# A hybrid transformer step: DMA stores begun on ScalarE, six load tiles for four, and one block inversion moved into the scan

## The chip, the cores and the metric

The kernel runs on one core of a Trainium2 chip. The metric is the device time of one execution in microseconds, median of three runs. The engines are called as the profile calls them: PE (TensorE), DVE (VectorE), ACT (ScalarE), POOL (GpSimd) and SP (SyncE, which here only begins DMAs).

## The reference, cut to what matters

Two trunk layers run over 128 context tokens and 1024 latent tokens of width 1024. Layer 0 has attention, layer 1 a bidirectional RWKV-7 mixer of 16 heads of 64; each ends with a squared-ReLU MLP. The change touches the mixer of layer 1 only:

```python
def wkv_scan(r, decay, k, v, kk, a, s0, reverse):
    def step(S, inp):
        r_t, w_t, k_t, v_t, kk_t, kka_t = inp
        sk = jnp.einsum('bhvk,bhk->bhv', S, kk_t)
        S = S * w_t[:, :, None, :] - sk[..., None] * kka_t[:, :, None, :] + v_t[..., None] * k_t[:, :, None, :]
        return S, jnp.einsum('bhvk,bhk->bhv', S, r_t)
    sf, ys = lax.scan(step, s0.astype(F32), seq, reverse=reverse)

def rwkv_mixer(h, p, s0):
    xr, xw, xk, xv, xa, xg = (h + xx * mu[n] for n in range(6))
    r = (xr @ w_rkv[0]).reshape(hs)
    k = (xk @ w_rkv[1]).reshape(hs)
    v = (xv @ w_rkv[2]).reshape(hs)
    g = jax.nn.sigmoid(xg @ g1) @ g2
    kk = (k * k_k).astype(F32)
    kk = kk * lax.rsqrt(jnp.sum(kk * kk, axis=-1, keepdims=True) + 1e-12)
    for d in range(2):
        wlog = -jax.nn.softplus(-(w0[d] + jnp.tanh(xw @ w1[d]) @ w2[d])) - 0.5
        decay = jnp.exp(-jnp.exp(wlog.astype(F32))).reshape(hs)
        a = jax.nn.sigmoid(a0[d] + (xa @ a1[d]) @ a2[d]).reshape(hs)
        kd = k * (1.0 + (a - 1.0) * k_a)
        y, sf = wkv_scan(r, decay, kd, v, kk, a, s0[:, d], reverse=(d == 1))
    ...
    out = (y.reshape(B, T, D) * g) @ w_o
```

## The kernel before, in words

All tokens are held as 1152 columns in three blocks of 384 (`TB`), the width as eight slices of 128 (`KD`); a slice holds two heads and is called a pair below. The scan is not run token by token but in 18 chunks of 64 tokens (`NC`), six (`NB`) to a block. Within a chunk the dependence of tokens on each other is a triangular matrix; its two 32x32 diagonal blocks are inverted by elimination (`invert`), the rest is products.

**`rwkv_proj` (about 2050 to 2775 us).** `dense` multiplies by the three weights in turn, k (i=1), r (i=0), v (i=2), in 24 pieces of one slice by one block each; a piece is 24 matmuls on PE, and its `done` function copies PSUM to an `ro` tile on ACT and stores it to DRAM: `out32` (L1114 to 1118) for k, r, v and the gate, `v_done` (L1203 to 1210) for v, which is also transposed and stored as `vtd`. During r and v, after every second piece, the generator `operands` (L1230) is advanced by one step. A step is one slice and one block, 24 in all: it loads k, kk and r from DRAM (`load`, L1223, tiles `ld`), multiplies kk on DVE (L1247), and for each direction builds the decay by tanh and exp on ACT (tiles `e` of `etiles`, or in three of four half-steps of the v phase slices of an idle activation buffer), a running sum on DVE (L1262), `ar` on POOL (L1270, 1271) and `bk` on DVE and POOL (L1278, 1279). It stores `ar` to `ard`, `bk` to `bkd`, and the masked diagonal blocks `nt`, which PE makes as `ng`, to `nd`. At a slice's last block `nd` becomes `self.tri[p8]`; for the first `PI` = 3 slices the pair's blocks are inverted at once (L1304): `invert` loads `iv`, runs 31 times two DVE operations (L1349, 1350), one ACT copy (L1352), and a store of `td` (L1354).

**`rwkv_scan` (about 2778 to 3502 us).** A list `plan` gives each generator's steps a due time and they are called in that order. For each pair p there are three `prepare`s (one per block), a `recurrence` of 54 steps and a `finish`; t = 27 p. The pairs with p >= `PI` are inverted at t-45 to t-25 (L1703), the context chunks' blocks (`KD`) at -12 to 8. `prepare` loads `ar`, `rp`, `bk` and, from `td`, the inverses `ta`; PE makes the 64x64 products `gp`, DVE masks them to `g` (L1454); then PE joins the diagonal inverses (`mp`, L1469, L1477) with ACT copies into `tt` (L1471). `recur` runs on two alternating pairs: PE `cp` (L1530), ACT `xt` (L1539), PE `cp` (L1546), ACT `mu` (L1548), PE `cp` (L1553), DVE sum (L1556).

**What orders the work.** All DMAs of these stages are begun on SP (`self.dma`). The framework's scheduler, which runs an own timeline, decides on which place of an engine's queue each instruction stands: an engine takes them strictly in that order. A tile pool with `bufs` buffers per tag makes a new tile wait for the last reader of the tile whose buffer it takes. Each DMA is put on one of eight lanes of semaphores (DMAHW0 to 7); the one that begins it first waits until the lane's previous DMA has landed.

The numbers that the change touches: `AB`, buffers of `ar` in `prepare` (L1425); `PI`; `EB`, buffers of `e` (L1221); `LB`, buffers of `ld` (L1224); and the `bufs=2` of `ta` (L1424).

Of the kernel before, what the change touches and what calls it, by code (L numbers as in the profile page):

```python
# [10 lines left out]
F32 = mybir.dt.float32  # L11
# [13 lines left out]
TB = 384  # L25
# [10 lines left out]
DW = (((1, "a"), (1, "b"), (2, "a")), ((2, "a"), (2, "b"), (3, "a")))  # L36
PVS = (2, 4)
GB = 8
AB = 4
GT = 22  # L40
MAN = 0
MB = 3
TTB = 5
SD = 0
YB = 3
PI = 3
PT = 27
EB, LB, KDE, OF, BKE = 7, 4, 1, 5, 1
PL = 13
NEK = 1  # L50
KO = 1
# [38 lines left out]
class Net:  # L90
    def __init__(self, tc, A, O, C):
        self.tc, self.nc = tc, tc.nc
        self.A, self.O, self.C = A, O, C
        nc = tc.nc
        self.V, self.S, self.G, self.T = nc.vector, nc.scalar, nc.gpsimd, nc.tensor
        self.dma = nc.sync.dma_start
        self.uid = 0

    def nm(self, s):
# [921 lines left out]
    def rwkv_proj(self, act, early, pool, pse, ps):  # L1021
        A, S, V, G, T, dma, dr = self.A, self.S, self.V, self.G, self.T, self.dma, self.dr
        KE = (V, G)[KDE]
        NC, NB = TOK // 64, 6
# [89 lines left out]
        def out32(dst, b, p):  # L1114
            o = pool.tile([128, TB], F32, tag="ro", name=self.nm("ro"), bufs=2)
            S.copy(o, p)
            dma(dst[:, b * TB : (b + 1) * TB], o)
            return o

        def head_sums(x, out):  # L1120
# [6 lines left out]
        def rows_out(out, src):  # L1127

            o, x = out.rearrange("k e (t p) -> (k e t) p", p=128), src.rearrange("p k e t -> p (k e t)")
            for i in range(0, x.shape[1], 72):  # L1130
                tp = pse.tile([128, HW], F32, tag="tp", name=self.nm("rtp"), bufs=3)[0:72, 0:128]
                T.transpose(tp, x[:, i : i + 72], self.ident)
                rt = load(None, "rt")[0:72, 0:128]
                S.copy(rt, tp)
                dma(o[i : i + 72], rt)

        def lowranks(n, hs, after):

# [63 lines left out]
        def v_done(p8, b, p):  # L1202
            o = out32(self.vd[:, p8], b, p)  # L1203
            for c in range(0, 6, 3):
                vp = pse.tile([128, HW], F32, tag="tp", name=self.nm("vp"), bufs=3)[0:64, 0:TB]
                for j in range(3):
                    T.transpose(vp[:, j * 128 : j * 128 + 128], o[:, (c + j) * 64 : (c + j) * 64 + 64], self.ident)
                vt = early.tile([128, TB], F32, tag="mix", name=self.nm("vt"), bufs=3)[0:64].rearrange("p (e c d) -> p e c d", e=2, d=64)
                S.copy(vt.rearrange("p e c d -> p c e d"), vp.rearrange("p (c e d) -> p c e d", e=2, d=64))
                dma(self.vtd[p8, :, :, 6 * b + c : 6 * b + c + 3], vt)  # L1210

        def etiles():

# [120 lines left out]
    def invert(self, pool, p):  # L1334
# [3 lines left out]
        V, S, dma, dr = self.V, self.S, self.dma, self.dr  # L1338
        n_ = self.tri[p]
        blocks = "a d c e i s t -> (a d c e i) s t" if p == KD else "d c e i s t -> (d c e i) s t"  # L1340

        both = pool.tile([128, 32, 2, 32], F32, tag="iv", name=self.nm("iv"), bufs=1)
# [8 lines left out]
            yield  # L1351
        S.copy(nb_, iv.rearrange("p x y -> p y x"))  # L1352
        t_ = self.tri[p] = dr.tile([*n_.shape[:-1], 2, 32], F32, name=self.nm("td"))
        dma(t_.rearrange(blocks.replace("s t", "s m t")), both)  # L1354


    def rwkv_scan(self, pool, late, ps, psl):
        A, S, V, G, T, dma, dr, O = self.A, self.S, self.V, self.G, self.T, self.dma, self.dr, self.O
        NC, NB = TOK // 64, 6
# [56 lines left out]
        def prepare(p, b, u):  # L1416

            for d in range(2):
# [2 lines left out]
                if self.tti[d] < TTB:  # L1421
                    G.memset(tt, 0.0)
                self.tti[d] += 1
                ta = u["ta", d, b] = pool.tile([128, NB, 2, 32], F32, tag="ta", name=self.nm("ta"), bufs=2)  # L1424
                ar = u["ar", d, b] = pool.tile([128, 3, NB, 64], F32, tag="ar", name=self.nm("ar"), bufs=AB)  # L1425
                bk = bks[self.bki % 2]
                rp = u["rp", d, b] = rps[self.rpi % GB]
# [57 lines left out]
        def recur(p, u, y):  # L1485

            k = p % 2
# [96 lines left out]
                T.transpose(fp[:, d], fm[:, d], self.ident)  # L1584
            S.copy(fs.rearrange("p d h k -> p d (h k)"), fp)
            for d in range(2):
                dma(O[6][0, 0, d, 2 * p : 2 * p + 2].rearrange("h v k -> v h k"), fs[:, d])

        def finish(p, y_):

# [300 lines left out]
```

## Time and profile before

| | us |
|---|---|
| three runs, median (lowest to highest) | 4452.35 (4450.34 to 4462.19) |
| the profiled execution, its own time | 4463.4 |
| its span in the profile | 4461.6 |
| PE busy (89% of the span) | 3987.0 |
| DVE busy (62%) | 2771.1 |
| ACT busy (38%) | 1711.8 |
| POOL busy (28%) | 1238.0 |

The profiled execution took 11.05 us more than the median of the three runs. The busy shares are means over stages that have different limits. The chain of waits that ended last, followed back from the end, is a PE chain (24% of the span on PE), and reaches back only to 3166 us; the stages that the change touches lie mostly ahead of that, so they are read from windows of time and from the waits of each engine in them.

### The profile page before, as it was taken

To read this page: it belongs to the slowest core of one execution; us is meant where nothing else is said; L and a number is where in the kernel's file an instruction comes from. 1 tells how busy PE (TensorE), PEld (TensorE's weight loads), DVE (VectorE), ACT (ScalarE), POOL (GpSimd) and SP (SyncE) were. 2 spreads that over 40 slices of the span, in tenths; PEclk is the share of its full clock that TensorE was granted. 3 is DMA by queue.
4 is the path that set the end of the run, shared out by engine and by line. 5 is a ranking of instruction groups with operands and counts; after the bars stand their busy time and mean duration, and the time that the engine had idled before them with its cause. 6 is when DMAs were issued, how large, how long until landed. Compare 5 with 4: busy or idle time off the path is not lost. (4 is left out here: it accounts for less than half of the span.)

```text
span 4461.6 us, 78674 instructions
## 1 busy us (share of the span) xinstructions
PE 3987.0 (89%) x30058; PEld 3386.6 (76%) x30058; DVE 2771.1 (62%) x5837; ACT 1711.8 (38%) x4041; POOL 1238.0 (28%) x1519
## 2 busy tenths in 40 slices
PE   6989998879999999978978686898898799999998
PEld 4767776667888888868966564676677589999997
DVE  6856788865766666675147885676653564444445
ACT  5436776543211121243344453354555342222122
POOL 1223557650000000024255575344444200000001
PEclk8999999889999999989988787898999699999999
DMA  4444223223222222221235666766553411111112
GB/s 163 128 139 119 76 73 89 79 68 124 77 73 70 74 79 67 75 98 47 100 110 142 168 206 168 168 149 153 137 143 104 175 62 48 38 48 43 43 38 99
DMA packets 558520, 452.36 MB, mean 101 GB/s; under 512 B 191302, under 2 KB 529214, under 8 KB 556990
## 3 DMA queue, kind: packets, MB, share of 16 engines
q1 hardware_dynamic: 558144, 447.33, 34.2%
q8 instruction: 238, 3.90, 0.4%
q14 instruction: 138, 1.13, 0.1%
HBM read 323.45 MB, written 123.76 MB: 100 GB/s over the span
## 5 line engine op out<-in xcount | busy, mean ns | idle before, releaser
L956 PE MATMUL acc<-w2h,f 128*128 128x512 f32 x2304 | 735.3, 393 | 4.8 <-ACT f L835 3.8
L936 PE MATMUL mp<-h_b,w1h 128*128 128x384 f32 x1536 | 521.9, 340 | 0.0
L936 PE MATMUL mp<-h_a,w1h 128*128 128x384 f32 x1536 | 517.1, 337 | 0.8 <-ACT h L300 0.7
L936 PE MATMUL mp<-h_a,w1l 128*128 128x384 f32 x1536 | 516.9, 337 | 0.0
L956 PEld LDWEIGHTS acc<-w2h,f 128*128 128x128 f32 x2304 | 433.1, 188 | 101.4 <-ACT f L835 5.5
L956 PE MATMUL acc<-w2l,f 128*128 128x512 f32 x1152 | 452.3, 393 | 0.0
L962 DVE TENSOR_TENSOR acc<-acc,acc 128x1024 f32<-128x1024 f32 x270 | 328.7, 1218 | 139.3 <-PE acc L956 136.9
L660 POOL TENSOR_TENSOR ptl<-pt,pth 128x512 fp32r<-128x512 f32 x192 | 248.2, 1294 | 219.8 <-DVE pth L659 129.0
L1453 PE MATMUL gp<-ar,bk 128*64 128x192 f32 x2304 | 290.7, 356 | 20.4 <-DMA bk<-bkd 11.5
L936 PEld LDWEIGHTS mp<-h_a,w1h 128*128 128x128 f32 x1536 | 288.5, 188 | 7.0 <-issue 2.0
L936 PEld LDWEIGHTS mp<-h_b,w1h 128*128 128x128 f32 x1536 | 289.0, 188 | 4.2 <-issue 0.7
L936 PEld LDWEIGHTS mp<-h_a,w1l 128*128 128x128 f32 x1536 | 289.2, 188 | 0.1
L938 ACT ACTIVATE mt<-mp 128x384 f32<-128x384 f32 x192 | 94.1, 490 | 501.2 <-PE mp L936 499.0
L1111 PE MATMUL rp<-mxh,pwh 128*128 128x384 f32 (+2 forms) x720 | 268.9, 374 | 10.2 <-POOL pwh L1102 6.1
L1111 PE MATMUL rp<-h_b,pwh 128*128 128x384 f32 (+2 forms) x720 | 261.2, 363 | 3.5 <-DVE h_b L1068 3.4
L988 POOL TENSOR_TENSOR acc<-acc,mraw 128x1024 f32<-128x1024 f32 x6 | 15.4, 2564 | 894.5 <-DVE mrv L110 887.9
L1111 PE MATMUL rp<-mxh,pwl 128*128 128x384 f32 (+2 forms) x720 | 258.4, 360 | 0.8 <-POOL pwl L1099 0.8
L956 PEld LDWEIGHTS acc<-w2l,f 128*128 128x128 f32 x1152 | 216.8, 188 | 44.9 <-issue 3.1
L1791 POOL MEMSET h_a<- 128x8 f32 x4 | 0.3, 113 | 901.3 <-PE mp L936 901.3
L1454 DVE TENSOR_TENSOR g<-gp,gm 128x384 f32<-128x384 f32 x288 | 157.6, 554 | 134.0 <-PE gp L1453 124.7
L940 DVE TENSOR_TENSOR mf<-mt 128x384 f32<-128x384 f32 x192 | 106.3, 553 | 214.4 <-ACT mt L938 214.4
L1453 PEld LDWEIGHTS gp<-ar,bk 128*64 128x64 f32 x2304 | 172.4, 146 | 45.7 <-DVE g L1454 10.7
(439 smaller groups left out, 9600.1 us busy)
## 6 DMA issues: line engine op xcount, KB each, us to landing
mraw<-in_mlp_w_dram SPq DMA_DIRECT2D x64, 1024.0 KB
adaw<-in_w_ada_dram SPq DMA_DIRECT2D x80, 512.0 KB
bkd<-bk SPq DMA_DIRECT2D x48, 384.0 KB
ard<-ar SPq DMA_DIRECT2D x48, 384.0 KB
q<-QSd SPq DMA_DIRECT2D x256, 64.0 KB
ar<-ard SPq DMA_DIRECT2D x40, 384.0 KB
praw<-in_rwkv_w_rkv_dram SPq DMA_DIRECT2D x24, 512.0 KB
x1d<-acc SPq DMA_DIRECT2D x18, 512.0 KB
```

The costliest lines, as they stand in the source:

```text
L660: (V if w < 4 else G).tensor_tensor(c["l"][:, g : g + w, o], t["tp", g][:, 0:w], f32(c["h"][:, g : g + w, o]), op=ALU.subtract)
L936: T.matmul(p, x[:, k, :], act[b].v[y][:, k], start=k == 0 and i == 0, stop=k == KD - 1 and i == 2)
L938: S.activation(t, p, AF.Relu)
L940: V.tensor_tensor(f, t, t, op=ALU.mult)
L956: T.matmul(p[:, hf], x[:, cols], y[:, n], start=j == 0 and i == 0, stop=j == 1 and i == 2)
L962: V.tensor_tensor(a, a, pf, op=ALU.add)
L988: (G if b < 2 else V).tensor_tensor(a, a, x1[t], op=ALU.add)
L1111: T.matmul(p, x[:, k, :], a[y][:, k], start=k == 0 and i == 0, stop=k == KD - 1 and i == 2)
L1453: T.matmul(gp[row(x), j].rearrange("p (a t) -> p a t", t=64), bk[e][:, x, q + j], ar[:, :, q + j], start=True, stop=True, tile_position=(0 ...
L1454: V.tensor_tensor(g[:, e].rearrange("p j a t -> p j (a t)"), gp, gm[:, d, e, None].to_broadcast([128, 2, 192]), op=ALU.mult)
L1791: net.G.memset(a.hx[:, :, z : z + 1], 0.0)
```

## The change

Three things are changed together.

First, 173 DMAs are begun by ACT (`nc.scalar.dma_start`) that were begun by SP: the stores of r and k (`rkd`, 48), of the gate (`gd`, 24), of v (`vd`, 24) and of its transpose (`vtd`, 48), the row sums (`kkd` 2, `bsd` 2), the inverses (`td`, 9) and the final states (16). SP keeps 1893 of its 2066. The stores of `ard`, `bkd`, `nd` and of the scan's output stay on SP.

Second, buffers: `ld` 4 to 6, `ta` 2 to 4, `e` 7 to 6, `ar` in the scan 4 to 3.

Third, `PI` 3 to 2: pair 2 is inverted in the scan's plan at t-45 to t-25 with t = 54, which is 9 to 29, rather than in the projections.

The counts of instructions on PE, DVE and POOL and of ACT's compute don't change. No PE instruction ahead of row 10508 of PE's 17,284 (rows of equal shape taken together) changes its place, and the last 4185 rows (the output projection and the last MLP) are the same.

```diff
-AB = 4
+AB = 3
...
-PI = 3
+PI = 2
...
-EB, LB, KDE, OF, BKE = 7, 4, 1, 5, 1
+EB, LB, KDE, OF, BKE = 6, 6, 1, 5, 1
...
         self.dma = nc.sync.dma_start
+
+        self.dma_s = nc.scalar.dma_start
...
             S.copy(o, p)
-            dma(dst[:, b * TB : (b + 1) * TB], o)
+            self.dma_s(dst[:, b * TB : (b + 1) * TB], o)
...
                 S.copy(rt, tp)
-                dma(o[i : i + 72], rt)
+                self.dma_s(o[i : i + 72], rt)
...
-                dma(self.vtd[p8, :, :, 6 * b + c : 6 * b + c + 3], vt)
+                self.dma_s(self.vtd[p8, :, :, 6 * b + c : 6 * b + c + 3], vt)
...
-        dma(t_.rearrange(blocks.replace("s t", "s m t")), both)
+        self.dma_s(t_.rearrange(blocks.replace("s t", "s m t")), both)
...
-                ta = u["ta", d, b] = pool.tile([128, NB, 2, 32], F32, tag="ta", name=self.nm("ta"), bufs=2)
+                ta = u["ta", d, b] = pool.tile([128, NB, 2, 32], F32, tag="ta", name=self.nm("ta"), bufs=4)
...
-                dma(O[6][0, 0, d, 2 * p : 2 * p + 2].rearrange("h v k -> v h k"), fs[:, d])
+                self.dma_s(O[6][0, 0, d, 2 * p : 2 * p + 2].rearrange("h v k -> v h k"), fs[:, d])
```

Line numbers of the changed kernel are higher by 2 from L98 on. Three places show how the instructions move.

**DVE, the operands' early steps.** Tiles kk_4375, kk_4408, kk_4473 are those of steps 1, 2 and 3. Before, from the last `bk` of step 1 to that of step 2's first half:

```order
L1278 SCALAR_TENSOR_TENSOR bk_4396_22217<-tha_4391_22201,en_4393_22205 128x384
L1247 SCALAR_TENSOR_TENSOR kk_4408_22320<-k_4407_22318,CB_103,kk_4408_22320 128x384
L1299 SCALAR_TENSOR_TENSOR kd_4384_22157<-r_4376_22134,CB_103,kd_4384_22157 128x384
L1292 TENSOR_TENSOR nt_4398_22246<-ng_4397_22221,nm_21929 128x192
L1262 SCALAR_TENSOR_TENSOR cum_4411_22326<-m01_19680,ec_4410_22325 128x390
L1125 COPY bss_21738<-hst_4399_22251 128x3x2
L1276 SCALAR_TENSOR_TENSOR tha_4413_22333<-tha_4413_22333,kk_4408_22320 128x384
L1278 SCALAR_TENSOR_TENSOR bk_4418_22349<-tha_4413_22333,en_4415_22337 128x384
```

Now, the rows from the last `bk` of step 0 on:

```order
L1280 SCALAR_TENSOR_TENSOR bk_4363_22028<-tha_4358_22012,en_4360_22016 128x384
L1301 SCALAR_TENSOR_TENSOR kd_4350_21966<-r_4342_21943,CB_103,kd_4350_21966 128x384
L1249 SCALAR_TENSOR_TENSOR kk_4408_22320<-k_4407_22318,CB_103,kk_4408_22320 128x384
L1294 TENSOR_TENSOR nt_4365_22057<-ng_4364_22032,nm_21929 128x192
L1127 COPY bss_21738<-hst_4366_22063 128x3x2
L1264 SCALAR_TENSOR_TENSOR cum_4378_22138<-m01_19680,ec_4377_22137 128x390
L1278 SCALAR_TENSOR_TENSOR tha_4380_22145<-tha_4380_22145,kk_4375_22132 128x384
L1280 SCALAR_TENSOR_TENSOR bk_4385_22161<-tha_4380_22145,en_4382_22149 128x384
```

The product kk of step n+1 stood right behind step n's last `bk`; now that of step n+2 stands there (kk_4408 behind step 0's bk_4363), so it runs a whole step ahead of its readers. The load of kk in SP's queue moves with it: kk_4473 stood behind step 2's first `bkd` store, and stands now behind step 1's last `ard` store.

**ACT, one step of the operands in the v phase.** The words in brackets are the semaphores that a row waits for (DMAHW0 to 7 are the lanes). Before:

```order
L1116 COPY ro_5009_25521<-rp_5008_25496 128x384 [waits DMAHW6_49,PE_49]
L1260 ACTIVATE es_4991_25378<-lp_4992_25380,hb_19683 128x384 [waits DMAHW1_49,DVE_49,PE_49]
L1264 ACTIVATE es_4991_25378<-lp_4993_25385,hb_19683 128x384
L1209 COPY vt_5011_25528<-vp_5010_25524 64x3x2x64 [waits DMAHW4_49,PE_49]
L1261 ACTIVATE es_4991_25378<-es_4991_25378 128x6x64 [waits Activation_49]
L1209 COPY vt_5013_25535<-vp_5012_25531 64x3x2x64 [waits DMAHW3_49,PE_49]
L1274 ACTIVATE es_4991_25378<-es_4991_25378,oka_19687,hb_19683 128x384 [waits Activation_49]
L1260 ACTIVATE es_4998_25431<-lp_4999_25433,hb_19683 128x384 [waits DMAHW5_49,DVE_49,Pool_49]
L1264 ACTIVATE es_4998_25431<-lp_5000_25438,hb_19683 128x384 [waits PE_49]
L1266 ACTIVATE es_4991_25378<-es_4991_25378 128x384 [waits DVE_49]
L1267 ACTIVATE es_4991_25378<-es_4991_25378 128x390 [waits Activation_49,Pool_49]
```

Now, at the same kind of place:

```order
L1211 COPY vt_4978_25429<-vp_4977_25425 64x3x2x64 [waits DMAHW0_49,PE_49]
L1211 COPY vt_4980_25436<-vp_4979_25432 64x3x2x64 [waits PE_49]
L1276 ACTIVATE es_4958_25279<-es_4958_25279,oka_19687,hb_19683 128x384 [waits Activation_49]
L1212 DMA vtd_19671<-vt_4978_25429 128x1x192 [waits DMAHW2_49,Activation_49]
L1266 ACTIVATE es_4965_25332<-lp_4967_25339,hb_19683 128x384 [waits PE_49]
L1212 DMA vtd_19671<-vt_4980_25436 128x1x192 [waits DMAHW4_49,Activation_49]
L1268 ACTIVATE es_4958_25279<-es_4958_25279 128x384 [waits DVE_49]
L1269 ACTIVATE es_4958_25279<-es_4958_25279 128x390 [waits Pool_49]
L1270 ACTIVATE Dc_11596<-es_4958_25279 128x6
L1268 ACTIVATE es_4965_25332<-es_4965_25332 128x384
L1269 ACTIVATE es_4965_25332<-es_4965_25332 128x390
L1270 ACTIVATE Dc_11596<-es_4965_25332 128x6
```

The two stores of vt and the one of ro stand between the tanh, exp and scaling operations of the operands, each with a wait for the ACT copy ahead of it and one for a DMA on its lane. Of the 173 stores 119 have such a lane wait, 102 of them for a DMA that SP began, most for `ard`, `bkd`, r, k and kk.

**PE, pair 2's first `prepare` in the scan.** mp_5517 is the product that reads the inverses of pair 2 (ta_5474) first. Before, and the row ahead of it:

```order
L1562 MATMUL yp_5448_28485<-g_5358_27750,mu_5406_28105 64x64
L1562 MATMUL yp_5448_28485<-g_5364_27791,mu_5406_28105 64x64 x2
L1453 MATMUL gp_5493_28827<-ar_5475_28730,bk01_27019 64x192 x4
L1469 MATMUL mp_5517_28982<-ta_5474_28729,g_5476_28739 32x32 x4
L1469 MATMUL mp_5517_28982<-ta_5474_28729,g_5485_28778 32x32
L1453 MATMUL gp_5499_28876<-ar_5497_28866,bk10_27020 64x192 x4
```

Now:

```order
L1555 MATMUL cp_5522_29017<-mu_5494_28849,g_5458_28541 64x64 x2
L1564 MATMUL yp_5504_28899<-g_5426_28330,mu_5494_28849 64x64
L1564 MATMUL yp_5504_28899<-g_5458_28541,mu_5494_28849 64x64 x2
L1548 MATMUL cp_5465_28600<-xt0_26961,tt03_26954 64x64 x2
L1548 MATMUL cp_5465_28600<-xt0_26961,tt13_26959 64x64 x2
L1471 MATMUL mp_5517_28982<-ta_5474_28729,g_5476_28739 32x32 x4
L1471 MATMUL mp_5517_28982<-ta_5474_28729,g_5485_28778 32x32 x4
L1471 MATMUL mp_5517_28982<-ta_5474_28729,g_5490_28817 32x32 x4
```

Before, it stood right behind the `gp` products of its own `prepare` (33 of the scan's 144 groups of `gp` stood ahead of it). Now 39 of them do, those of its `prepare` and the next half among them, and it stands behind rows of both running recurrences. On DVE the elimination of pair 2 now stands between `g` number 48 and number 70 of 288, where pair 3's stood (50 to 72); pair 3's moves to 78 to 89, ahead of where its first reader stands (108) by 19.

## Rows read from the trace of the kernel before

**Rows 1.** Windows: length, busy us of PE, PEld, DVE, ACT, POOL; clock, DMA share, GB/s.

```profile
2250.00:2550.00 300.00, 227.62 (x1929) 189.05 (x1927) 199.66 (x315) 131.91 (x279) 164.09 (x162) 0.83 0.49 138
2300.00:2350.00 50.00, 43.33 (x363) 35.99 (x360) 13.56 (x21) 16.30 (x35) 21.40 (x23) 0.80 0.45 135
2550.00:2600.00 50.00, 36.09 (x368) 28.62 (x368) 48.19 (x77) 21.87 (x48) 31.85 (x32) 0.76 0.64 196
2550.00:2780.00 230.00, 164.14 (x1984) 131.32 (x1984) 156.87 (x216) 106.45 (x238) 153.09 (x165) 0.79 0.62 189
2800.00:3500.00 700.00, 617.80 (x10483) 489.24 (x10483) 392.97 (x1045) 338.96 (x1111) 288.58 (x666) 0.90 0.55 135
```

**Rows 2.** Waits of DVE, 2255 to 2780 us: total us, times, longest.

```profile
DVE kk L1247 <- DMA kk<-kkd: 76.0, 19, 8.6
```

**Rows 3.** Timeline of DVE, two early steps: start, us, operation, [idle before].

```profile
2304.91 0.62 DVE L1247 SCALAR_TENSOR_TENSOR kk<-k,CB,kk 128x384 f32<-128x384 f32 x1 [6.71 <-DMA kk<-kkd]
...
2322.54 0.68 DVE L1276 SCALAR_TENSOR_TENSOR tha<-tha,kk 128x384 f32<-128x384 f32 x1 [2.05 <-ACT kd L1274]
2323.25 1.18 DVE L1278 SCALAR_TENSOR_TENSOR bk<-tha,en 128x384 f32<-128x384 f32 x1
2331.03 0.62 DVE L1247 SCALAR_TENSOR_TENSOR kk<-k,CB,kk 128x384 f32<-128x384 f32 x1 [6.60 <-DMA kk<-kkd]
2331.56 0.61 DVE L1299 SCALAR_TENSOR_TENSOR kd<-r,CB,kd 128x384 f32<-128x384 f32 x1
```

**Rows 4.** Timeline of SP in the second of them.

```profile
2323.28 0.54 SPq L1245 DMA_DIRECT2D kk<-kkd  x1
```

**Rows 5.** Waits of POOL, 2255 to 2780 us.

```profile
POOL ar L1270 <- DMA k<-rkd: 9.8, 1, 9.8
...
POOL ar L1271 <- DMA r<-rkd: 7.1, 1, 7.1
```

**Rows 6.** Waits of PE, 2255 to 2780 us.

```profile
PE hst L1124 <- DVE es L1299: 42.2, 11, 9.8
PE ng L1290 <- DVE bk L1278: 22.9, 9, 5.2
PE hst L1124 <- DVE kd L1299: 22.3, 7, 6.1
```

**Rows 7.** Three starts of kk on DVE around the third inversion.

```profile
2550.95 0.62 DVE L1247 SCALAR_TENSOR_TENSOR kk<-k,CB,kk 128x384 f32<-128x384 f32 x1 [5.40 <-DMA kk<-kkd]
...
2619.03 1.19 DVE L1247 SCALAR_TENSOR_TENSOR kk<-k,CB,kk 128x384 f32<-128x384 f32 x1 [2.84 <-DMA kk<-kkd]
...
2671.64 0.79 DVE L1247 SCALAR_TENSOR_TENSOR kk<-k,CB,kk 128x384 f32<-128x384 f32 x1 [3.29 <-POOL es L1298]
```

**Rows 8.** Windows of L1349, then L1350, in the third inversion: DVE busy us.

```profile
2540.00:2620.00 80.00, 18.96 (x31) 0.77 0.65 188
...
2540.00:2620.00 80.00, 20.38 (x31) 0.77 0.65 188
```

**Rows 9.** Source view of SP, 2000 to 2800 us: L1117 and L1210, durations in ns.

```profile
L1117 SPq DMA_DIRECT2D rkd<-ro x48: 319/320/2659, 2098.4 to 2434.4; - x48
...
L1210 SPq DMA_DIRECT2D vtd<-vt x48: 508/556/1749, 2465.9 to 2750.5; - x48
```

**Rows 10.** Waits of ACT, 2255 to 2780 us.

```profile
ACT vt L1209 <- DMA vtd<-vt: 8.0, 2, 7.7
```

**Rows 11.** Waits of ACT, 2800 to 3500 us.

```profile
ACT tt L1471 <- DMA ta<-td: 105.6, 33, 12.0
```

**Rows 12.** Waits of PE, 2800 to 3500 us.

```profile
PE yp L1562 <- ACT mu L1548: 20.3, 19, 5.4
PE cp L1546 <- ACT xt L1539: 19.0, 17, 5.6
PE mp L1469 <- DMA ta<-td: 9.7, 1, 9.7
```

**Rows 13.** Timeline of ACT: end of pair 3's inversion.

```profile
2923.87 1.96 ACT L1352 COPY iv<-iv 128x1024 f32<-128x1024 f32 x1
```

## The prediction

> **What bounds the kernel now.** I read the windows of time first, to see which engine is full in which stage, then each engine's waits in the two stages that the change touches, then a few steps one by one. The chain of waits is of no use here: it reaches back only to 3166 us.
>
> In the projections' stretch with the operands (2250 to 2780 us) no engine is full for long [rows 1]: PE is busy 227.6 of 300 us and then 164.1 of 230, so 138 us of it are idle in all, DVE 199.7 and 156.9, ACT 131.9 and 106.5. The bound moves: from 2300 to 2350 us PE is busy 43.3 of 50 us and DVE 13.6, while from 2550 to 2600 us, under an inversion, DVE is busy 48.2 and PE falls to 36.1. The reader is to see a chain that passes from load to DVE to PE and back: DVE waits 76.0 us in 19 places for the load of kk [rows 2], and PE waits 42.2 + 22.3 + 22.9 = 87.4 us for DVE's products behind it [rows 6]. PE's granted clock averages 0.83 and 0.79 in these two windows, a mix of its levels of 2.4 and 1.2 GHz, against 0.90 in the scan, where PE is fuller [rows 1]; what a fuller PE would get back in clock has no term.
>
> In the scan (2800 to 3500 us) PE is busy 617.8 of 700 us [rows 1], so 82 us are idle at most. ACT waits 105.6 us in 33 places for the loads of `ta` [rows 11], and PE waits 20.3 + 19.0 us behind ACT's copies and 9.7 us for `ta` itself [rows 12].
>
> **The change part by part.** Gains have a minus.
>
> *kk's load, 4 to 6 `ld` tiles.* Before, the load of kk is begun at 2323.28 us [rows 4] and DVE uses it at 2331.03 [rows 3]: 7.75 us, of which the last `bk` of the step before covers 1.18 and the wait is 6.60. Now the load goes out behind the last `ard` store, and kk's product behind the product of bonus sums (L1301). Between issue and use then lie `tha` (0.68), `bk` (1.18), that product (0.61) and, I take, half of the 2.05 us that `tha` waits for ACT: 3.5 us in all. What is left to wait is 4.3 us for 6.6, 35% less, and 35% of 76.0 is **-27**. From both sides: 0, if the load's buffer comes free no earlier against its use than now; -76, if it lands in time every time. I take the value near the low end, since load and use moved ahead together, a full step each.
>
> *k and r.* POOL waits 9.8 us for k and 7.1 us for r, once each [rows 5]; with two more tiles both loads go out sooner. **-10**, between -17 and 0.
>
> *The third inversion.* Its 62 operations take DVE 18.96 + 20.38 = 39.3 us [rows 8]. The four steps that it lies in take 2619.03 - 2550.95 = 68.1 us, the four after it 2671.64 - 2619.03 = 52.6 us [rows 7]: **-15.5**; between -39, all of it, and 0, if the later steps are short for another reason. In the scan it lies beside DVE's other work, where DVE is busy 393.0 of 700 us [rows 1], so its operations are covered; its lateness has a term below. If that cover went, it would give back up to 39 us.
>
> *Stores begun by ACT.* A store of r, k or v costs the beginning engine 0.32 us, one of `vtd` 0.556 [rows 9]. In the v phase that is 24 x 0.32 + 48 x 0.556 = 34.4 us on ACT, which is busy 106.5 of 230 us [rows 1], 46%. With that share of it on the path it is **+15**. Queued behind a store on ACT are the tanh and exp of the operands, for which DVE's running sum and POOL's `ar` wait; what a lane wait adds there is the second rival. From below: ACT waits 8.0 us, 7.7 of them once, for `vt` tiles whose stores SP had not begun [rows 10]; with ACT itself beginning them that can go, so -8 to +78 (worked out with that rival). SP loses those issues, but it is no bound: it took kk's load within 0.03 us of the start of the `bk` beside it [rows 3, 4].
>
> *`e` tiles 7 to 6.* Matters in the first nine steps, 18 half-steps, where all half-steps use these tiles. The spare tile lets the next half-step start one operation early; nearest row is `bk` with 1.18 us [rows 3], so 0 to 18 x 1.18 = +21. I take **+5**: the reader that holds the tile, POOL's `ar`, runs ahead of `bk`.
>
> *`ta` 2 to 4.* At most the 20.3 + 19.0 + 9.7 = 49 us by which PE waits behind ACT or `ta` [rows 12], at least nothing. **-15**, a third: many of the 33 waits are for an inverse that has just been stored, which buffers don't hasten.
>
> *`ar` 4 to 3 in the scan.* Loads of `ar` start a half later; the nearest row of a late load is PE's one wait for `ta`, 9.7 us [rows 12]. 0 to +20 (two of them), taken as **+5**.
>
> *Pair 2's inverse late.* Its elimination takes the place in DVE's order where pair 3's stood. That one ended with an ACT copy at 2923.87 + 1.96 = 2925.8 us [rows 13]; a store and a load follow, at kk's 7.75 us each about 2941. Pair 2's first `mp` stood at `g` 66 of 288, six before pair 3's last operation at 72; at 700 / 288 = 2.4 us a `g` that was about 2909, so it comes some 30 us later. PE has `gp` of two halves and two recurrences to run meanwhile: 0 to +30, taken as **+6**, near the low end for that cover. What is late next is the ACT copies to `tt` of that pair, and its recurrence.
>
> *Stores of `td` and final states on ACT.* 22 after the second inversion, at 0.32 us [rows 9]: 0 to +7, **+2**.
>
> The sum: -27 - 10 - 15.5 + 15 + 5 - 15 + 5 + 6 + 2 = **-34.5 us**. Against the profiled execution's 4463.4 us that is 4428.9. The profiled execution was 11.05 us above the median of the runs, 4452.35, so on that I forecast 4417.9, rounded **4418**.
>
> **The rivals.**
>
> *All loads hidden.* If six tiles take kk, k and r off DVE's and POOL's path, the terms are -76 and -17 for -27 and -10: -34.5 - 56 = -90.5, 4362 us. For it: 87.4 us of PE's waits lie behind DVE's chain [rows 6], and 138 us of PE are idle. Against: kk's use in DVE's order moved as far ahead as its load.
>
> *ACT stalls at its stores: slower.* Place: the v phase. A store waits on ACT until its lane's earlier DMA has landed, and 102 of the 119 lane waits are for DMAs that SP began, which take up to kk's 7.75 us. From 2550 to 2780 us ACT has 230 - 106.5 = 123.5 us free. Of the 72 v stores that begin in the 285 us from 2465.9 to 2750.5 [rows 9] some 58 fall there, with 28 us of issue, so 96 us or 1.65 us a store can be lost before ACT is full. At a mean wait of 3 us ACT is 58 x 3 - 96 = 78 us over; in place of the +15 above the sum is -34.5 - 15 + 78 = +28.5, 4481 us. It decides from 58 x 2.5 = 145 us of lane waits on, a mean of 2.5 us. For it: ACT is in order, and the operands of DVE and POOL stand behind. Against: the lane's earlier DMA is eight begins back, mostly landed.
>
> *No change.* kk's product waits as before, because the loads gain nothing: 0 for -27, so -7.5 or 4445 us. For it: 7.75 us lie between begin and use however SP is filled, and SP's queue is not what holds the load [rows 3, 4].
>
> The Trainium skill has a rule that speaks for this one ("DMA: Bandwidth & Descriptors", section "Issuing engines are not separate DMA queues"): beginning DMAs on several engines saves only the sequencer's time to begin them, as all run on the same 16 engines. By it the move of the stores alone would be worth nothing to the loads, which the row of kk's load bears out as far as it goes.
>
> **How the numbers follow.** Chances: the forecast 0.42, all hidden 0.18, ACT stalls 0.17, no change 0.23. The likeliest case alone runs from 4395 to 4440 by the ends of its small terms. The range for 8 in 10 goes on down into the case of hidden loads and up to near the slower rival: 4365 to 4475 us. A measurement of this kernel tells 0.3%, 13 us, from no change, so faster is below 4439 and slower above 4466. Faster: all of the hidden loads' 0.18, 0.40 of the forecast and 0.03 of no change, 0.61. Same: 0.18 of no change, 0.02 of the forecast, 0.01 of ACT's stalls, 0.21. Slower: 0.16 of ACT's stalls and 0.02 of no change, 0.18.
>
> **What would show it.** In the changed profile DVE's wait for kk should be near 50 us (near 10 by the first rival, 76 by the third); the four steps that held the inversion should take about 53 us; ACT should show no wait for the store of `vt`; ACT's lane waits ahead of its stores should sum to under 50 us (over 145 by the second rival); in the scan ACT's wait for `ta` should fall from 105.6 to some 70 us, with one long wait for pair 2's. The prediction is wrong if the operands' stretch does not get shorter by 30 us or so, or if the scan gets longer by more than 15.

## The result, and the profile after

The changed kernel takes 4436.06 us (median of 8 runs, 4430.76 to 4440.16), the kernel before 4460.59 us in the same series (8 runs, 4450.34 to 4469.76). The ratio is 0.9946, 95% interval 0.9933 to 0.9959: faster by about 24 us. One execution of a kernel further down (the best version, 4623.2 us at a granted clock of 0.81, where its others have 0.93 to 0.94) was in a slow state and is in none of the times and ratios. The forecast was 4418 us, 34.5 us less than before; of the two profiled executions the changed one spans 32.6 us less (4429.0 for 4461.6). The sum came out near the forecast; several of the terms of which it was made did not, and the runs below are about that.

The page of the changed kernel: its span, the busy time of the engines, and a DMA queue that the kernel before does not have.

```profile
span 4429.0 us, 78546 instructions
...
PE 3958.8 (89%) x30058; PEld 3373.4 (76%) x30058; DVE 2748.4 (62%) x5837; ACT 1711.2 (39%) x4041; POOL 1237.2 (28%) x1519
...
q10 hardware_dynamic: 24672, 33.71, 2.3%
```

The queue q10 is new and carries ACT's stores, 33.7 of the 447 MB. The engines' work is the same in kind and count; PE's busy time fell from 3987.0 to 3958.8 us, while the mean granted clock of the two profiled executions rose from 0.929 to 0.937.

Where the time went is read best from one line: the recurrence's first product `cp`, whose first and last start mark when the scan's recurrences begin and end. The source view of that line, before, then after (durations in ns, first and last start in us):

```profile
L1530 PE MATMUL cp<-mu,g x1152: 219/222/369, 2804.1 to 3497.3; 128*64 128x64 f32 x192
```

```profile
L1532 PE MATMUL cp<-mu,g x1152: 219/222/368, 2773.2 to 3465.0; 128*64 128x64 f32 x192
```

The first `cp` comes 30.9 us earlier, the last 32.3: all but 1.4 us of the gain lies ahead of the scan, and the scan from first to last `cp` takes 691.8 us for 693.2. The windows of the same stretches as [rows 1], same columns:

```profile
2250.00:2550.00 300.00, 224.97 (x2023) 186.22 (x2022) 206.32 (x322) 138.90 (x294) 174.44 (x172) 0.84 0.51 148
2300.00:2350.00 50.00, 47.01 (x415) 38.50 (x414) 16.67 (x27) 20.33 (x43) 27.83 (x26) 1.00 0.52 152
2550.00:2600.00 50.00, 39.25 (x490) 30.45 (x490) 30.30 (x39) 23.60 (x53) 39.27 (x40) 0.88 0.67 201
2550.00:2780.00 230.00, 168.72 (x2060) 133.88 (x2062) 125.51 (x200) 100.11 (x232) 149.00 (x173) 0.81 0.68 190
2800.00:3500.00 700.00, 602.97 (x10113) 480.94 (x10108) 417.42 (x1083) 342.64 (x1101) 285.54 (x639) 0.90 0.57 141
```

In the early steps, 2300 to 2350 us, PE is busy 47.0 of 50 us for 43.3 and its granted clock is 1.00, that is 2.4 GHz throughout, for 0.80, a mix with 1.2 GHz. Under the place where the third inversion was, 2550 to 2600, DVE's 48.2 us became 30.3. In the last window the scan had begun by 2773.

DVE's waits in 2255 to 2780 us, after; the first answers to [rows 2]:

```profile
DVE kk L1249 <- DMA kk<-kkd: 88.9, 22, 10.1
...
DVE nt L1294 <- PE ng L1292: 6.2, 4, 3.9
```

DVE's wait for kk did not fall from 76.0 to 50, as forecast; it is 88.9. (Of such a difference some 14 us can be chance: the kernel c below, whose projections hold the same operations of DVE in the same order as before, has 62.3.) What fell is its wait for PE's `ng`, which in the kernel before was

```profile
DVE nt L1292 <- PE ng L1290: 26.1, 5, 8.4
```

and PE's waits for DVE's products, 29.9 + 24.6 + 8.3 = 62.8 us for [rows 6]'s 87.4:

```profile
PE ng L1292 <- DVE bk L1280: 29.9, 11, 6.0
PE hst L1126 <- DVE es L1301: 24.6, 10, 5.0
...
PE hst L1126 <- DVE kd L1301: 8.3, 5, 4.8
```

An early step shows both. DVE's timeline, after, answering to [rows 3]:

```profile
2301.59 0.62 DVE L1249 SCALAR_TENSOR_TENSOR kk<-k,CB,kk 128x384 f32<-128x384 f32 x1 [4.82 <-DMA kk<-kkd]
...
2307.81 0.36 DVE L1294 TENSOR_TENSOR nt<-ng,nm 128x192 f32<-128x192 f32 x1 [0.80 <-PE ng L1292]
2311.26 0.97 DVE L1264 TENSOR_TENSOR_SCAN cum<-m,ec 128x390 f32<-128x390 f32 x1 [3.09 <-POOL ec L1261]
...
2318.83 0.62 DVE L1301 SCALAR_TENSOR_TENSOR kd<-r,CB,kd 128x384 f32<-128x384 f32 x1 [2.98 <-POOL ec L1261]
2324.06 0.62 DVE L1249 SCALAR_TENSOR_TENSOR kk<-k,CB,kk 128x384 f32<-128x384 f32 x1 [4.61 <-DMA kk<-kkd]
```

and SP's begin of that step's kk:

```profile
2316.76 0.58 SPq L1247 DMA_DIRECT2D kk<-kkd  x1
```

The step from kk to kk is 2324.06 - 2301.59 = 22.5 us; before it was 2331.03 - 2304.91 = 26.1. The wait for kk inside it is 4.61 us for 6.60, close to the 4.3 that was worked out, and 7.3 us still lie between the load's begin and its use. A larger change is another: `nt` now waits 0.80 us for `ng`. In the kernel before the same `nt`, of the step's second half, was:

```profile
2319.25 0.36 DVE L1292 TENSOR_TENSOR nt<-ng,nm 128x192 f32<-128x192 f32 x1 [6.98 <-PE ng L1290]
```

There PE had a dense piece ahead of `ng` in its queue: `ng` began at 2318.58 us, 6.3 us after the `bk` that it reads was done. Of these 6.2 us less for `ng` and 2.0 less for kk only 3.6 are left in the step, since DVE now waits 3.09 and 2.98 us for POOL's `ec`, where it had no such wait.

### The profile page after: what moved, and what is told of

Read it like the earlier page. It is cut to its first block, busy times and chain, and to the rows that moved or that the text cites. A ratio compares the mean times of both kernels' runs of the same rounds, so it can differ in the third digit from the quotient of the medians.

```text
span 4429.0 us, 78546 instructions
## 1 busy us (share of the span) xinstructions
PE 3958.8 (89%) x30058; PEld 3373.4 (76%) x30058; DVE 2748.4 (62%) x5837; ACT 1711.2 (39%) x4041; POOL 1237.2 (28%) x1519
## 5 line engine op out<-in xcount | busy, mean ns | idle before, releaser
L990 POOL TENSOR_TENSOR acc<-acc,mraw 128x1024 f32<-128x1024 f32 x6 | 15.3, 2558 | 894.1 <-DVE mrv L112 887.5
L1456 DVE TENSOR_TENSOR g<-gp,gm 128x384 f32<-128x384 f32 x288 | 157.3, 554 | 105.6 <-PE gp L1455 98.3
```

Of the source, the lines that this page charges most:

```text
L1456: V.tensor_tensor(g[:, e].rearrange("p j a t -> p j (a t)"), gp, gm[:, d, e, None].to_broadcast([128, 2, 192]), op=ALU.mult)
```

## The experiments

All ratios are to the kernel before in the same series. There are three series, each on another chip, with five to twelve executions of each kernel: one for the four kernels with one part undone, one for the four with one part alone, one for the pairs and the last experiment. The edits are named by a letter each: **s**, stores begun by ACT; **t**, the projections' tiles (`ld` 6, `e` 6); **c**, the scan's tiles (`ta` 4, `ar` 3); **p**, pair 2 inverted in the scan (`PI` 2). The changed kernel is s+t+c+p.

| kernel | ratio (95%) | first cp, us | scan, first to last cp, us |
|---|---|---|---|
| before | 1 | 2804.1 | 693.2 |
| p | 1.0006 (0.9995 to 1.0018) | 2791.6 | 691.2 |
| s | 1.0008 (0.9996 to 1.0021) | 2813.2 | 680.9 |
| t | 1.0002 (0.9991 to 1.0014) | 2801.0 | 692.5 |
| c | 0.9988 (0.9977 to 0.9999) | 2807.6 | 670.9 |
| t+c | 0.9963 (0.9951 to 0.9976) | 2800.4 | 672.0 |
| s+c | 0.9964 (0.9951 to 0.9976) | 2809.6 | 662.2 |
| s+t | 0.9967 (0.9955 to 0.9979) | 2781.6 | 685.7 |
| s+t+c | 0.9928 (0.9907 to 0.9948) | 2783.7 | 669.7 |
| t+c+p | 0.9952 (0.9936 to 0.9969) | 2794.9 | 672.9 |
| s+c+p | 0.9970 (0.9956 to 0.9984) | 2796.0 | 676.4 |
| s+t+p | 0.9965 (0.9951 to 0.9978) | 2772.6 | 695.6 |
| s+t+c+p | 0.9946 (0.9933 to 0.9959) | 2773.2 | 691.8 |

The last two columns are from one profiled execution of each kernel. How far they can be trusted is seen in the five pairs of rows that differ by c alone, which changes tiles of the scan only: their first `cp` differ by 0.6 to 3.6 us. The stretch behind the last `cp`, which no edit was meant to touch, takes 963.9 to 971.7 us in these kernels. And p's profiled execution, 4454.4 us, was the fastest of its twelve, whose median is 4462.7.

### One part undone

The inversion back in the projections (s+t+c):

```diff
-PI = 2
+PI = 3
```

> The changed kernel with PI = 3 again: pair 2's inversion is back in the projections, all else as changed. The changed kernel stands at 0.9946 of before. Theory 1 (the inversion's removal from the projections is the largest term, and costs nothing in the scan): 10 to 16 us come back, all between 2500 and 2780 us, ratio 0.997 to 0.998; first cp of the scan 10 to 16 us later than the changed kernel's 2773.2. Rival 1 (the inversion is covered in both places; the tiles and stores carry the gain): ratio 0.994 to 0.996. Rival 2 (pair 2's late inverse costs the scan as much as the projections gain): ratio 0.994 to 0.996 with first cp 10 us later and the scan 10 us shorter.

It ran in 4425.44 us, 0.9928: none of the 10 to 16 us of theory 1 came back, and the ratio is 1.8 parts in a thousand, 8 us, under the changed kernel's, though the two intervals touch. The first `cp` is 10.5 us later, in the range of theory 1, but the scan is 22.1 us shorter:

```profile
L1532 PE MATMUL cp<-mu,g x1152: 219/222/371, 2783.7 to 3453.4; 128*64 128x64 f32 x192
```

That is rival 2's kind, and more than it asked. Why the projections gave less than the inversion's 39 us is seen in five steps of DVE's kk. With the inversion beside them (s+t+c):

```profile
2542.00 0.61 DVE L1249 SCALAR_TENSOR_TENSOR kk<-k,CB,kk 128x384 f32<-128x384 f32 x1
...
2554.84 0.61 DVE L1249 SCALAR_TENSOR_TENSOR kk<-k,CB,kk 128x384 f32<-128x384 f32 x1
...
2568.01 0.59 DVE L1249 SCALAR_TENSOR_TENSOR kk<-k,CB,kk 128x384 f32<-128x384 f32 x1
...
2584.47 0.60 DVE L1249 SCALAR_TENSOR_TENSOR kk<-k,CB,kk 128x384 f32<-128x384 f32 x1
...
2597.26 1.02 DVE L1249 SCALAR_TENSOR_TENSOR kk<-k,CB,kk 128x384 f32<-128x384 f32 x1
...
2618.86 0.62 DVE L1249 SCALAR_TENSOR_TENSOR kk<-k,CB,kk 128x384 f32<-128x384 f32 x1 [4.39 <-DMA vtd<-vt]
```

and in the changed kernel, with none:

```profile
2539.85 0.62 DVE L1249 SCALAR_TENSOR_TENSOR kk<-k,CB,kk 128x384 f32<-128x384 f32 x1 [4.25 <-DMA kk<-kkd]
...
2553.30 0.62 DVE L1249 SCALAR_TENSOR_TENSOR kk<-k,CB,kk 128x384 f32<-128x384 f32 x1 [1.93 <-DMA kk<-kkd]
...
2564.57 0.62 DVE L1249 SCALAR_TENSOR_TENSOR kk<-k,CB,kk 128x384 f32<-128x384 f32 x1 [2.58 <-DMA vtd<-vt]
...
2578.66 0.62 DVE L1249 SCALAR_TENSOR_TENSOR kk<-k,CB,kk 128x384 f32<-128x384 f32 x1 [4.68 <-DMA kk<-kkd]
...
2595.30 1.30 DVE L1249 SCALAR_TENSOR_TENSOR kk<-k,CB,kk 128x384 f32<-128x384 f32 x1 [2.54 <-DMA kk<-kkd]
...
2610.64 0.62 DVE L1249 SCALAR_TENSOR_TENSOR kk<-k,CB,kk 128x384 f32<-128x384 f32 x1 [5.27 <-DMA kk<-kkd]
```

The first four steps take 55.3 us with the inversion's operations on DVE and 55.4 without. With them DVE is busy for 54.7 us of that, without them for 34.0, and it waits at the kk of each step, three times for kk's load and once for `vtd`, 11.7 us in all. The fifth step, in which the inversion ends, does get shorter, from 21.6 to 15.3 us. Over the stretch DVE's wait for kk in s+t+c is

```profile
DVE kk L1249 <- DMA kk<-kkd: 48.7, 14, 9.4
```

so taking some 39 us of work off DVE [rows 8] put 40 us of waiting there, 88.9 for 48.7. In all five pairs of kernels with and without p this wait is longer with p, by 22 to 47 us.

The stores back on SP (t+c+p):

```diff
-        self.dma_s = nc.scalar.dma_start
+        self.dma_s = nc.sync.dma_start
```

> The changed kernel with all 173 stores begun by SP again. Theory 1 (the forecast's term: a store on ACT costs its issue, 15 us on the path in the v phase, and gives the loads nothing): faster than the changed kernel by some 15 us, ratio about 0.991. Rival 1 (SP's queue held loads behind stores that waited for ACT's copies, and that is the gain): 15 to 30 us come back, ratio 0.998 to 1.001, with DVE's wait for kk and ACT's wait for vt longer. Rival 2 (neutral, both terms small): 0.994 to 0.996.

0.9952, rival 2: neutral in time. But not stage by stage: the first `cp` comes 21.7 us later and the scan is 18.9 us shorter than in the changed kernel. In the projections that is what rival 1 asked, with DVE's wait for kk at 98.8 us, though ACT's wait for the stores of `vt` did not come back.

The projections' tiles as before (s+c+p):

```diff
-EB, LB, KDE, OF, BKE = 6, 6, 1, 5, 1
+EB, LB, KDE, OF, BKE = 7, 4, 1, 5, 1
```

> The changed kernel with 4 ld tiles and 7 e tiles again. Theory 1 (the forecast's terms for kk, k, r and e: -27, -10, +5): 32 us come back, ratio about 1.002. Rival 1 (DVE's wait for kk did not shrink in the changed kernel, 88.9 us for 76.0, so the tiles are worth nothing): ratio 0.994 to 0.996. Rival 2 (the tiles gain not through the wait for kk but through the order: ng ahead of the dense products on PE in the first nine steps, where DVE's wait for ng fell from 26.1 to 6.2 us): 10 to 20 us come back, ratio 0.997 to 0.999, and DVE's wait nt<-ng is over 20 us again.

0.9970: 11 us came back, at the low end of rival 2 and with intervals that touch. DVE's wait of `nt` for `ng` is 18.8 us again, just short of the 20 that this rival asked. Theory 1's 32 us did not come back.

The scan's tiles as before (s+t+p):

```diff
-AB = 3
+AB = 4
...
-                ta = u["ta", d, b] = pool.tile([128, NB, 2, 32], F32, tag="ta", name=self.nm("ta"), bufs=4)
+                ta = u["ta", d, b] = pool.tile([128, NB, 2, 32], F32, tag="ta", name=self.nm("ta"), bufs=2)
```

> The changed kernel with the scan's tiles as before: ta 2, ar 4. Theory 1 (the forecast's terms -15 and +5): 10 us come back, all in the scan, ratio about 0.997, ACT's wait for ta about 100 us again. Rival (the scan is bound by the recurrence and PE, and ta's loads by the inverses, not the buffers; it took 692 us in both kernels): ratio 0.994 to 0.996, though ACT's wait for ta is long again.

0.9965: 8 us came back by the ratio, where theory 1 asked 10, though with intervals that touch, and in the profile only 3.8 us of it lie between first and last `cp`; the stretch behind the last `cp` is 7.7 us longer, inside its scatter in the other kernels.

### One part alone, on the kernel before

The same four edits, each made alone on the kernel before.

p alone:

```diff
-PI = 3
+PI = 2
```

> The kernel before with PI = 2 alone: pair 2's inversion moves to the scan, nothing else. Theory now (from the changed kernel with PI = 3: first cp 10.5 us later, scan from first to last cp 22.1 us shorter, in all 8 us faster): the move gains 10 to 16 us in the projections and costs the scan more; ratio 1.000 to 1.004, first cp near 2790, scan over 700 us. Rival (the inversion's 39 us on DVE are worth 15 us in the projections and nothing in the scan, as forecast): ratio 0.996 to 0.997, scan 693 us.

1.0006: no gain from the move. The first `cp` comes 12.5 us earlier, as expected; the scan is not longer here (691.2 us, in a profile that was 8.3 us faster than the kernel's median). DVE's wait for kk rose at once, from 76.0 to

```profile
DVE kk L1247 <- DMA kk<-kkd: 98.1, 20, 8.5
```

s alone: the five `dma(...)` stores of the change's diff as `self.dma_s(...)`, with

```diff
+        self.dma_s = nc.scalar.dma_start
```

> The kernel before with the 173 stores begun by ACT alone. Theory now (neutral, as with the stores back on SP in the changed kernel, 0.9952 for 0.9946): ratio 0.998 to 1.001; if first cp is 10 to 20 us earlier, the scan is as much longer. Rival (the forecast's term of +15 us on ACT): ratio 1.003 to 1.004, first cp some 15 us later. Rival (stores held loads up in SP's queue): ratio 0.993 to 0.997.

1.0008, neutral as expected, with the first `cp` 9.1 us later and the scan 12.3 us shorter, the reverse of the case that the expectation named. DVE's wait for kk fell to 56.6 us, with four `ld` tiles, and the projections got no shorter by it.

t alone:

```diff
-EB, LB, KDE, OF, BKE = 7, 4, 1, 5, 1
+EB, LB, KDE, OF, BKE = 6, 6, 1, 5, 1
```

> The kernel before with 6 ld and 6 e tiles alone. Theory now (from the changed kernel with 4 and 7: 11 us came back, and DVE's wait for ng rose from 9 to 34 us): ratio 0.996 to 0.998, DVE's wait for ng from 36 us to under 20, the wait for kk not under 60. Rival (the forecast's -27 - 10 + 5 through the wait for kk): ratio 0.992 to 0.993, wait for kk near 50. Rival (the tiles are worth something only with the stores on ACT): ratio 0.999 to 1.001.

1.0002: the third expectation held, the tiles alone are worth nothing. The wait for `ng` did fall, from 35.9 to 18.0 us (`nt` and `es` together), and the wait for kk stayed at 79.6. SP still waited for ACT's copies ahead of its stores of r and v, 30.4 us for 34.7 in the kernel before:

```profile
SPq L1117 <- ACT ro L1116: 30.4, 13, 6.6
```

c alone:

```diff
-AB = 4
+AB = 3
...
-                ta = u["ta", d, b] = pool.tile([128, NB, 2, 32], F32, tag="ta", name=self.nm("ta"), bufs=2)
+                ta = u["ta", d, b] = pool.tile([128, NB, 2, 32], F32, tag="ta", name=self.nm("ta"), bufs=4)
```

> The kernel before with ta 4 and ar 3 alone. Theory now (from the changed kernel with 2 and 4: 8 us came back): ratio 0.997 to 0.999, first cp at before's 2804, scan under 690 us, ACT's wait for ta near 40 us for 117. Rival (the scan gains nothing, 693 us, since PE waits little for ACT's ta copies): ratio 0.999 to 1.001.

0.9988, at the upper end of theory's range. Its interval takes in the rival's too, so the scan decides: it shrank to 670.9 us, more than expected; ACT's wait for `ta`, 105.6 us in [rows 11], is

```profile
ACT tt L1471 <- DMA ta<-td: 41.4, 12, 12.6
```

### Two parts together

Four single edits add up to +0.4 parts in a thousand, and together give -5.4: some must work only together.

t+c, which is the changed kernel with

```diff
-PI = 2
+PI = 3
...
-        self.dma_s = nc.scalar.dma_start
+        self.dma_s = nc.sync.dma_start
```

> Tiles of the projections (ld 6, e 6) and of the scan (ta 4, ar 3) together, stores on SP, pair 2 inverted in the projections. Alone they gave 1.0002 and 0.9988. Theory now (what gains is the two sets of tiles together, and the stores' engine is neutral): 0.992 to 0.995. Rival 1 (terms add up): 0.998 to 1.000. Rival 2 (the tiles need the stores off SP): 0.998 to 1.000, while the kernel with stores and scan tiles is near 0.998 too.

s+t, the changed kernel with

```diff
-AB = 3
+AB = 4
...
-PI = 2
+PI = 3
...
-                ta = u["ta", d, b] = pool.tile([128, NB, 2, 32], F32, tag="ta", name=self.nm("ta"), bufs=4)
+                ta = u["ta", d, b] = pool.tile([128, NB, 2, 32], F32, tag="ta", name=self.nm("ta"), bufs=2)
```

> Stores on ACT and the projections' tiles together, the scan's tiles as before, pair 2 inverted in the projections. Alone they gave 1.0008 and 1.0002. Theory now: 0.998 to 1.001, since the scan's tiles are missing. Rival (stores off SP are what lets six load tiles work): 0.993 to 0.996, first cp near 2783 as in the kernel with all but the inversion's move.

s+c, the changed kernel with

```diff
-PI = 2
+PI = 3
...
-EB, LB, KDE, OF, BKE = 6, 6, 1, 5, 1
+EB, LB, KDE, OF, BKE = 7, 4, 1, 5, 1
```

> Stores on ACT and the scan's tiles together, the projections' tiles as before, pair 2 inverted in the projections. Alone they gave 1.0008 and 0.9988. Theory now (stores neutral, terms without the ld tiles add up): 0.998 to 1.000. Rival (stores on ACT free SP for the scan's loads, 0.9970 with the inversion moved too): 0.994 to 0.997, scan under 672 us.

All three pairs came out alike: 0.9963, 0.9967, 0.9964. So t+c is less than theory hoped, the stores' engine is not neutral beside t (1.0002 and 0.9967, though 0.9952 and 0.9946 with c and p beside it), and no pair is the only one that matters. The stages tell more than the times. The first `cp` is at 2781.6 us in s+t and 2783.7 in s+t+c, and nowhere else with `PI` 3 under 2800:

```profile
L1532 PE MATMUL cp<-mu,g x1152: 219/222/370, 2781.6 to 3467.3; 128*64 128x64 f32 x192
```

With s alone it is 9.1 us later, with t alone 3.1 earlier, with both 22.5 earlier. That gain of the two together does not depend on c: from c to s+t+c it is 23.9 us. DVE's wait for kk in s+t is the shortest of all these kernels:

```profile
DVE kk L1249 <- DMA kk<-kkd: 42.8, 12, 9.8
```

against 56.6 with s alone and 79.6 with t alone. So in the projections s and t need each other. SP's waits fit this reading: with SP beginning the stores, a load that has a free tile can stand in SP's queue behind a store that waits for ACT; with four tiles, a free queue has no tile to load into. SP's wait ahead of kk's load for `tha`, a last reader of an `ld` tile, is in the kernel before and with s alone

```profile
SPq L1245 <- DVE tha L1276: 30.7, 10, 5.3
```

```profile
SPq L1247 <- DVE tha L1278: 40.2, 11, 6.2
```

With t it is gone there, while with t alone the 30.4 us of waiting for ACT's copies shown above are left; s+t has neither. (Ahead of the loads of k and r SP's waits for DVE and POOL grow with six tiles: 91 us with t alone for 48 in the kernel before.) That this is why s and t need each other is argued from these rows; no run tests it by itself.

In the scan, c takes 22.3 us off alone, 20.5 with t, 18.7 with s, 16.0 with s and t: much the same term each time. With s, t and p it takes off only 3.8.

### The inverse earlier

The scan's loss from the moved inversion, 22.1 us between s+t+c and the changed kernel, could come from pair 2's inverse being late or from DVE's added work. In this kernel the two inversions are due 8 earlier:

```diff
-        put(self.invert(pool, KD), 32, -12, 8)
+        put(self.invert(pool, KD), 32, -20, 0)
...
-                put(self.invert(pool, p), 32, t - 45, t - 25)
+                put(self.invert(pool, p), 32, t - (53 if p == 2 else 45), t - (33 if p == 2 else 25))
```

> The changed kernel with pair 2's inversion due 8 earlier in the scan's list (1 to 21), and that of the context blocks 8 earlier too, so that its inverse is ready sooner. Theory 1 (the move costs the scan about 20 us because pair 2's inverse is late): 8 us or more come off the changed kernel, ratio 0.991 to 0.9935, scan from first to last cp under 680 us for 691.8. Rival (it costs since 39 us more of DVE work lie in the scan, wherever they stand): 0.994 to 0.996, scan 685 to 695 us.

0.9944 (0.9931 to 0.9956) and a scan of 692.5 us, the numbers of the rival. But the edit did less than it was meant to: the ACT copy that ends pair 2's inversion starts at 2879.87 us for 2883.93 in the changed kernel, 4.1 us sooner, so that this run tells little.

```profile
L1532 PE MATMUL cp<-mu,g x1152: 219/222/369, 2771.6 to 3464.1; 128*64 128x64 f32 x192
```

What speaks against the lateness is in the runs already shown. The first product of a recurrence is `sp`; here are those of pair 0 and pair 2 in the changed kernel,

```profile
2770.84 0.36 PE L1517 MATMUL sp<-ident,s 64*128 64x64 f32 x1 [0.15 <-DMA s<-in_state_rwkv_dram]
...
2948.19 0.27 PE L1517 MATMUL sp<-ident,s 64*128 64x64 f32 x1
```

and in s+t+c:

```profile
2780.08 0.37 PE L1517 MATMUL sp<-ident,s 64*128 64x64 f32 x1 [0.15 <-DMA s<-in_state_rwkv_dram]
...
2956.12 0.27 PE L1517 MATMUL sp<-ident,s 64*128 64x64 f32 x1
```

Pair 2's recurrence begins 177.4 us after pair 0's with the late inverse and 176.0 us with the early one. Of the 22.1 us that the scan loses, 1.3 have been lost by then, and the rest comes bit by bit: at the first `sp` of pairs 3 to 7 the lag is 3.8, 7.2, 12.7, 16.8 and 21.4 us, though pair 2's inversion has ended by 2886 us.

## Why the prediction was right or wrong

**The time.** Forecast 4418 us in a range of 4365 to 4475, faster with 0.61; measured 4436. The forecast of -34.5 us met a measured -24.5. Neither of its two signs of being wrong came: the first `cp`, which ends the operands' stretch, is 30.9 us earlier, and the scan is 1.4 us shorter. The nearness is in part luck, since terms that were wrong went different ways: kk's wait did not fall, the inversion's move gained nothing in time, and the stores, which were to cost 15 us, gained beside the tiles. The step that failed is the crediting of terms to single edits: the largest gain needs two of them at once, and the inversion's gain in the projections was given back in the scan.

**kk's load, `ld` tiles.** The step by step working was right where it was made: 4.3 us of wait forecast, 4.61 measured in an early step. What failed was to carry that 35% over the whole 76.0 us and to give it to the tiles. The wait over the stretch did not fall, because the moved inversion no longer fills it; with `PI` 3 (s+t) it fell to 42.8, below the 50 forecast. Nor is the wait's sum a price: with s alone it was 19.4 us shorter, and the first `cp` 9.1 us later. And the tiles alone gave nothing (1.0002); the forecast saw SP as no bound because it took the load at once, [rows 4], in the one step it looked at. (That load began 0.06 us behind the end of `tha`, a last reader of an `ld` tile: a tile may have held it.)

**Stores on ACT.** Forecast +15 us. Alone they cost nothing that the ratio tells (1.0008, 0.9996 to 1.0021). The sign depends on the tiles: with four `ld` tiles the first `cp` comes 9.1 us later with them (before, s) or 2.0 (c, s+c); with six it comes earlier, by 19.4 (t, s+t), 16.7 (t+c, s+t+c) and 21.7 us (t+c+p, changed). For that gain the forecast had no term. In the ratio it is 3.5 parts in a thousand from t to s+t and from t+c to s+t+c, and 0.6 with p beside it. The rival of ACT stalling did not come. In the source view of `vtd`'s store the longest begin took 1134 ns, and one operation behind, ACT's `en`, waited for such a store, for 2.4 us. ACT's timeline from 2050 to 2800 us has in all some 5 us in which ACT stood idle right ahead of a store, for 145 us that the rival needed; the longest is that ahead of the second row here, 2.65 us.

```profile
L1212 ACTq DMA_DIRECT2D vtd<-vt x48: 515/524/1134, 2455.5 to 2728.7; - x48
...
  ACT en L1268: 2.4, 1
```

```profile
2564.12 0.48 ACT L1118 COPY ro<-rp 128x384 f32<-128x384 f32 x1 [1.53 <-PE rp L1113]
2567.25 0.33 ACTq L1119 DMA_DIRECT2D vd<-ro  x1
```

**k and r.** Of the two single waits of 9.8 and 7.1 us k's is gone and r's is still there once, 7.5 us. They were never tested alone; k's is gone with t alone and with s alone.

**The third inversion.** Forecast -15.5 us in the projections and +6 in the scan. The first `cp` came earlier with the move in all five pairs of kernels, by 5.5 to 13.6 us (12.5 for p alone, 10.5 from s+t+c), so the term's size there was somewhat high. It failed in the scan, where I wrote that DVE's operations are covered because DVE is busy 393 of 700 us. With stores on ACT the move lengthens the scan in each of three pairs: s+c 662.2 to 676.4, s+t 685.7 to 695.6, s+t+c 669.7 to 691.8. With stores on SP it does not (693.2 to 691.2, 672.0 to 672.9). In time the move is worth nothing that is clear of the intervals: in five pairs of kernels with and without it, in parts of a thousand, +0.6, -1.1, +0.6, -0.2, +1.8. One reading is that a share of idle time is no cover for an operation that stands ahead of a recurrence's own: DVE's sum (L1558) releases POOL's `sd`, and that ACT's `mu`. ACT's wait for `sd` was 15.0 us before and, in the changed kernel and in s+t+c, is

```profile
ACT mu L1550 <- POOL sd L1538: 43.2, 23, 7.8
ACT tt L1473 <- DMA ta<-td: 29.0, 10, 6.1
```

```profile
ACT mu L1550 <- POOL sd L1538: 24.6, 20, 7.0
```

That wait grew with the move, but t+c+p has it too (41.9 us from 2790 to 3460) with a scan of 672.9 us, so that reading is not shown, and why the scan loses only when ACT begins the stores is left open. One thing in the traces goes with the loss, the place of the last pair's inversion in DVE's order. It ends at `g` 182 of 288 in s+t+c and at 207 in the changed kernel, at 184 and 204 in s+c and s+c+p, at 200 and 208 in s+t and s+t+p; with stores on SP the move leaves it in place, 203 and 207 (before, p), 206 and 203 (t+c, t+c+p). So the move sets the later inversions back just where the scan loses; no run tests whether that is the cause. That pair 2's inverse is late, the mechanism that I priced, accounts for 1.3 us at the start of that pair.

**`ta` and `ar`.** Forecast -15 + 5 = -10 us. The scan's term is -16 to -22 us with `PI` 3, and the ratio moved by -1.2 to -4.4 parts in a thousand, 5 to 20 us, wherever c was added; beside s, t and p the scan's term is only -3.8 us. With `PI` 3 I undersized the loads' part. In the changed kernel PE's waits that answer to [rows 12] are

```profile
PE yp L1564 <- ACT mu L1550: 27.6, 22, 5.8
PE cp L1548 <- ACT xt L1541: 9.6, 15, 2.3
...
PE mp L1471 <- DMA ta<-td: 4.5, 2, 2.8
```

and ACT's wait for `ta` is 29.0 us for 105.6, where 70 were forecast.

**What stays open.** In the profiled stages the pairs s+c and t+c are about the sums of their parts, but in the ratios each pair gains 3 to 4 parts in a thousand more than the two single edits. The singles and the pairs ran in different series, each against its own runs of the kernel before, and the profiles are of one execution each, so this difference isn't explained here. Every edit also gives all engines a new order after row 10508 of PE; what is put down to an edit is the edit with its order.

The best version of those run is by its ratio s+t+c, the change without the inversion's move: 4425.44 us, 0.9928 (0.9907 to 0.9948, which touches the changed kernel's interval).

## What to carry to other kernels

Taking work off an engine that waits for a load anyway can uncover the wait instead of saving time: before crediting a removed operation, look at what the engine would wait for next in the same steps. More load buffers and a free issuing queue were two halves of one edit here: each tried alone showed no gain in time. And a busy share of 56% did not show that DVE could take more work in the scan for nothing; what the scan lost by it depended on the other edits, and the runs do not say by which path.

## What the runs showed that I had not expected

PE's granted clock over 2300 to 2350 us went from 0.80 to 1.00, all 2.4 GHz, as PE's busy time in that window rose from 43.3 to 47.0 us. In another window it went the other way: from 2400 to 2450 us PE's busy time fell from 37.2 to 29.2 us and its clock from 0.86 to 0.74, so that over 2250 to 2550 us the clock gave back next to nothing (0.83 to 0.84). And the stores on ACT hardly cost ACT anything: a `vtd` store takes 524 ns to begin at the median and 48 of them stand between ACT's operations, but ACT's wait for the stores of `vt` (7.7 us once, [rows 10]) is gone, and ACT stood idle ahead of its stores for only some 5 us, though 119 of the 173 stores have a lane to wait for.
